# A hybrid attention layer with expert retrieval: 44 scatters per head instead of 48, and a second set of split weights in the activation stage

## The chip, the cores and the metric

One Trainium2 chip, one of its cores. The time of a kernel is the device time of one launch in microseconds (us), and the median of several runs is what counts. Profiles come from one further execution with the hardware profiler on. The engines are TensorE (PE; its weight loads are PEld), VectorE (DVE), ScalarE (ACT), GpSimd (POOL) and SyncE (SP), which only issues transfers here.

## The reference

A layer for 512 tokens and 16 meta tokens at width 2048: 8 heads of stick-breaking attention and 8 of forgetting attention, an output projection, then retrieval of experts by product keys. The last part takes nearly all the time and all of the change:

```python
def block(hb):
    q = (hb @ w_query).reshape(PEER_BLOCK, PEER_HEADS, 2, D_KEY // 2)
    s = jnp.einsum('thpc,hpnc->thpn', q, sub_keys)
    ...
    best_s, best_j = lax.top_k(cand_s, PEER_TOPK)
    idx = jnp.take_along_axis(cand_i, best_j, axis=-1)
    g = jax.nn.softmax(best_s, axis=-1)
    u_sel = jnp.take(u, idx, axis=0)
    a = jax.nn.gelu(jnp.einsum('thkd,td->thk', u_sel, hb), approximate=False)
    v_sel = jnp.take(v, idx, axis=0)
    return jnp.einsum('thk,thkd->td', (g * a).astype(hb.dtype), v_sel)
```

Each token has 8 heads with 16 experts each, out of 16384 = 128 x 128. Everything is float32.

## The kernel before

Float32 products are made from two halves: a weight tile `wr` is cast to a high half `wh` (ScalarE, L190) and the rest `wl` is subtracted (VectorE, or GpSimd where told, L191), and three matmuls give the product.

**Two ways for two kinds of tokens.** The first 160 tokens (128 "full" ones and 32 more, the x set) fetch the rows of their own experts: one gather per expert slot (`ahead`, L844, an indirect DMA on GpSimd's queue, 128 rows of 16 KB with u and v, 2 MB) into `grf`, of which there are two buffers. Then VectorE makes a dot with the token (L858), ScalarE makes the coefficient (L876, L877), and VectorE accumulates the v part (L864). The other 352 tokens (TD) are done densely: all 16384 experts in 128 blocks of 128.

**The stages of the dense part** are a list of items in order. `("A", j)` for j = 26 to 127: 48 matmuls of 352 columns (L1032) into `pa`, GELU on ScalarE (L903), stored to `a_scr`. `("D", j)` for j = 0 to 15: the same, but multiplied with the gate values `gg` read from `g_scr`, split into `ph` and `pl`. Then 256 V items with 24 matmuls each (L1046), between them the R items that bring activations and gates back. In iteration t the kernel issues loads for three items ahead, cuts item t + 1 into halves (`cut_up`) and issues the matmuls of item t. An item's weights are four quarters; `wh` and `wl` have four buffers each, so a quarter of the next item is cut when TensorE has read that quarter of the item before.

**The gate table.** `g_scr` in HBM holds a gate per (expert, dense token). It is zeroed early and filled by scatters: `total` (L951, VectorE) sums the gates of equal experts of a token into one column of `tot`, and a scatter (L963, an indirect DMA on GpSimd's queue) writes the 128 values of a column of `tot` to the places in a column of `dst`. Tokens 128 to 511 are three blocks of 128 (NDB); per head 3 x 16 = 48 columns, 8 heads, so 384 scatters. The first 32 partitions of block 0 are the x set; they need no table, so their `dst` points behind the table. `scatter` is a generator; each step makes one total of head h and one scatter of head h - 1, and iterations take 4 or 5 steps by turns (`NSC`).

**Order.** TensorE, VectorE, ScalarE and SyncE keep the order in which the code is written; GpSimd's queue is ordered by the scheduler when the program is built. In an iteration the steps of the gathers (`due(WA)`) and of the scatters stand between the four splits. Every queue is served in order, so what stands behind a waiting instruction waits too.

Of the kernel before, what the change touches and what calls it, by code (L numbers as in the profile page):

```python
# [9 lines left out]
F32 = mybir.dt.float32  # L10
F32R = mybir.dt.float32r
# [9 lines left out]
P = 128  # L21
# [3 lines left out]
D = 2048  # L25
KD = D // P
NH = 8
NTB = T // P
TOPK = 16
PH = 8  # L30
X = 32
TD0 = P + X
TD = T - TD0
NDB = NTB - 1
NG = P // X
# [6 lines left out]
GATES = 1  # L42
WA = 1.9
JC = 16
LEAD = JC // 2 + 1
NSC = (4, 5)
AHEAD = 3


# [46 lines left out]
def hymba_peer(ctx: ExitStack, tc: tile.TileContext, xT, w_in, w_fl, b_fg, g_mix, g_q, g_k, g_merge,  # L96
               w_out, g_ffn, w_q, keysT, uT, uv, out):
    nc = tc.nc

    def pool(name, bufs=1, **kw):  # L100
        return tc.tile_pool(name=name, bufs=bufs, **kw)

    cst = ctx.enter_context(pool("cst"))
    wp = ctx.enter_context(pool("wp", 3))
# [34 lines left out]
                            base=0, channel_multiplier=1)  # L139
# [4 lines left out]
                            base=-P, channel_multiplier=-1)  # L144
# [3 lines left out]
                            base=0, channel_multiplier=1)  # L148
# [4 lines left out]
                            base=0, channel_multiplier=1)  # L153
# [70 lines left out]
    with ExitStack() as fctx:  # L224
# [9 lines left out]
        with ExitStack() as actx:  # L234
# [16 lines left out]
            for k in range(KD):  # L251
                if k % 8 == 0:
                    wr = wp.tile([P, KD // 2, P], F32, name=f"wr_q0_{k}", tag="wr", bufs=2)
                x = raw.tile([P, S], F32, name=f"xr{k}", tag="raw")
# [8 lines left out]
                if k % 4 == 0:  # L263
                    wh = wp.tile([P, 4, P], F32R, name=f"wh_q0_{k}", tag="wh", bufs=4)
                    wl = wp.tile([P, 4, P], F32R, name=f"wl_q0_{k}", tag="wl", bufs=4)
# [12 lines left out]
                b = big.tile([P, S], F32R, name=f"hl{k}", tag="hl")  # L278
# [11 lines left out]
            for i, (lo, hi) in enumerate(KV):  # L290
                pm = pj(f"pss{i}")
                nc.tensor.matmul(pm[:, :264], ones, ssq[:, lo:hi], start=True, stop=True)
                y = rsqrt(t2, pm[:, :264], D, [P, 264], f"n{i}")
# [349 lines left out]
        with ExitStack() as mctx:  # L643
# [65 lines left out]
            first = [project(w_out[c], mh, ml, [(0, T)], f"wo{c}", hfs=(0,)) for c in range(3)]  # L709
# [178 lines left out]
    def due(n, hold=False):  # L888
        done[1] += n
        want = 0 if hold else min(nwork, int(nwork * done[1] / (0.975 * (WA * (P - NAP - GATES - 1) + 2 * P))))  # L890
        r = range(done[0], max(want, done[0]))
        done[0] = r.stop
        return [gens[i + 1] for i in r]
# [5 lines left out]
    dst = gp.tile([P, NDB, P], I32, name="dst")  # L899
    tot = gp.tile([P, NDB, P], F32, name="tot")  # L900
    def act_out(j, ps, keep=False):
        g = dn.tile([P, TD], F32, name=f"ga{j}", tag="ga", bufs=4)
        nc.scalar.activation(g, ps[:, :TD], AF.Gelu)  # L903
        if keep:
            return g
        nc.sync.dma_start(a_scr[j], g)

    def gates():
        e = gp.tile([P, NTB, P], F32, name="e")
        es = gp.tile([P, 2, NTB * PH], F32, name="es")  # L910
        ev = e.rearrange("p b (h k) -> p (b h) k", k=TOPK)
        nc.scalar.activation(e, res[:, :, 2, :], AF.Exp)
        nc.vector.reduce_sum(es[:, 0], ev, axis=AX.X)
        nc.vector.reciprocal(es[:, 1], es[:, 0])
        nc.vector.tensor_tensor(ev, ev, es[:, 1].unsqueeze(2).to_broadcast([P, NTB * PH, TOPK]), op=OP.mult)
        nc.vector.tensor_copy(g0, e[:, 0, :])
        nc.vector.scalar_tensor_tensor(ef, res[:, :, 1, :], float(P), res[:, :, 0, :], op0=OP.mult, op1=OP.add)
        nc.vector.tensor_copy(idx0, ef[:, 0, :])
        idxt = gp.tile([X, P], I32, name="idxt")
        nc.vector.tensor_copy(idxt, ef[:X, 1, :])  # L920
        for i in range(NG):
            for t, src in ((idx1, idxt), (g1, e[:X, 1, :])):
                nc.sync.dma_start(t[i * X:i * X + X], src[:, i * SL:i * SL + SL])
            nc.sync.dma_start(rxx[i * X:i * X + X], rx)
        for b in range(NDB):
            nc.vector.tensor_scalar(dst[:, b, :], ef[:, b + 1, :], float(TD), tcol[:, b:b + 1], op0=OP.mult, op1=OP.add)
        nc.gpsimd.iota(dst[:X, 0, :], pattern=[[1, P]], base=P * P * TD, channel_multiplier=P)
        return e

    act_out(JC, pa[0])  # L930
# [7 lines left out]
    psO = ctx.enter_context(pool("psO", 1, space=PSUM))  # L938
    wx = ctx.enter_context(pool("wx", 2))
    gt = ctx.enter_context(pool("gt", 2))  # L940
    pq = ctx.enter_context(pool("pq", 2))

# [2 lines left out]
    def scatter():  # L947
        def total(h, b, i):
            s, w = h * TOPK + i, (h + 1) * TOPK
            junk = gp.tile([P, P], F32, name=f"junk{h}{b}{i}", tag="junk")  # L950
            nc.vector.scalar_tensor_tensor(junk[:, :w], ef[:, b + 1, :w], ef[:, b + 1, s:s + 1],  # L951
                                           gts[:, b + 1, :w], op0=OP.is_equal, op1=OP.mult,
                                           accum_out=tot[:, b, s:s + 1])

        slots = [(b, i) for b in range(NDB) for i in range(TOPK)]
        for h in range(PH + 1):
            head = []
            for b, i in slots:
                if h < PH:
                    total(h, b, i)  # L960
                if h > 0:
                    s = (h - 1) * TOPK + i
                    w = nc.gpsimd.indirect_dma_start(  # L963
                        out=g_flat, out_offset=bass.IndirectOffsetOnAxis(ap=dst[:, b, s:s + 1], axis=0),
                        in_=tot[:, b, s:s + 1], in_offset=None)
                    for x in head:
                        tc.declare_no_dep(w.ins, x.ins, reason="the experts of one head differ")
                    head.append(w)
                yield
# [9 lines left out]
                items.append(("R", c * JC + x // 2 + LEAD))  # L979
            items.append(("V", c * JC + jj, half))  # L980

    ga, gg, raw_w, cut, pp, po, ppool = {}, {}, {}, {}, {}, {}, {}
    count = [0, 0]

    def kind(t):
        return items[t][0] if 0 <= t < len(items) else ""

    def load_gates(t):
        if kind(t) not in ("R", "D"):
            return  # L990
        j = items[t][1]
        if kind(t) == "R":
            ga[j] = dn.tile([P, TD], F32, name=f"gb{j}", tag="gb", bufs=3)
            nc.sync.dma_start(ga[j], a_scr[j])
        gg[j] = dn.tile([P, TD], F32, name=f"gg{j}", tag="gg", bufs=3)
        nc.sync.dma_start(gg[j], g_tab[j])

    def load(t):
        if t >= len(items):
            return  # L1000
        it = items[t]
        j = it[1]
        parts = [(f"u{x}", uT[j][:, x * 8:x * 8 + 8, :]) for x in range(2)] if it[0] != "V" else \
            [(f"v{it[2]}", uv[j * P:j * P + P, D + it[2] * H:D + it[2] * H + H])]
        raw_w[it] = []
        for nm, src in parts:
            w = (wp, wx)[count[0] % 2].tile([P, KD // 2, P], F32, name=f"wr_{nm}_{j}", tag="wr", bufs=2)
            count[0] += 1
            nc.sync.dma_start(w if it[0] != "V" else w.rearrange("p a b -> p (a b)"), src)
            raw_w[it].append(w)  # L1010

    def cut_up(it, lo_eng=None, work=()):
        r = []
        for n, w in enumerate(raw_w.pop(it)):
            for x in range(2):
                wh = wp.tile([P, 4, P], F32R, name=f"wh_{it[0]}{n}{x}_{it[1]}", tag="wh", bufs=4)
                wl = wp.tile([P, 4, P], F32R, name=f"wl_{it[0]}{n}{x}_{it[1]}", tag="wl", bufs=4)
                split(wh, wl, w[:, x * 4:x * 4 + 4, :], lo_eng)
                r.append((wh, wl))
                settle()  # L1020
                if it[0] != "V":
                    for _ in range(-(-len(work) // (5 - len(r)))):
                        next(work.pop(0), None)
        cut[it] = r
# [27 lines left out]
        return g  # L1052

    def high(j, g):
        ph = pq.tile([P, TD], F32R, name=f"ph{j}", tag="ph", bufs=2 * LEAD)
        nc.scalar.copy(ph, g)
        return g, ph

    def low(j, g, ph):
        pl_ = pq.tile([P, TD], F32R, name=f"pl{j}", tag="pl", bufs=2 * LEAD)  # L1060
        nc.vector.tensor_tensor(pl_, g, ph.bitcast(F32), op=OP.subtract)
        pp[j] = ph, pl_

# [23 lines left out]
    with tc.manual_schedule(engines=fixed):  # L1087
        sc = scatter()
        loaded = 0
        held = ()  # L1090
        for t in range(len(items) + 1):
            load_gates(t + 3)
            while t < len(items) and loaded < len(todo) and loaded <= rank[t] + AHEAD:
                load(todo[loaded])
# [4 lines left out]
                add_up(prev)  # L1099
            if prev[0] == "A":  # L1100
                act_out(prev[1], ga.pop(prev[1]))
            if prev[0] == "D":
                ga[prev[1]] = act_out(prev[1], ga.pop(prev[1]), True)
                g = gated(prev[1])
                low(prev[1], *high(prev[1], g))
# [3 lines left out]
                gts = gates()  # L1109
            work = []  # L1110
            if kind(t) in ("A", "D") and t > GATES:
                work = due(WA) + [sc] * NSC[t % 2]
            elif kind(t) == "V":
                work = due(1, hold=items[t][1] % JC == JC - 1 and t < len(items) - JC)
            if nxt.get(t) is not None:
# [83 lines left out]
```

## Time and profile before

| | |
|---|---|
| median of 3 runs | 3365.06 us (3356.91 to 3369.4) |
| profiled execution | 3352.32 us, its span 3350.6 us |
| mean TensorE clock granted | 0.987 |
| busy share of the span | PE 97%, PEld 91%, DVE 74%, POOL 42%, ACT 40% |
| A items (1303 to 2202 us) | 899 us of the span |

Busy matmul time overlaps itself, since matmuls are pipelined; what an item costs is read from how many matmuls pass in a stretch. The clock is a share of 2.4 GHz; 0.5 is the lower level of 1.2 GHz. "Idle before" an instruction is time in which its engine did nothing, and the name behind it is what ended that time, as inferred from semaphores.

### The profile page before, as it was taken

The page shows a single profiled execution, that of the slowest core. Times are in us where ns is not written, and L with a number is a line of the kernel's source. Part 1 is how long each engine was busy: PE and PEld are TensorE (multiplying, and loading weights), DVE is VectorE, ACT ScalarE, POOL GpSimd, SP SyncE. Part 2 cuts the span into 40 slices and gives each one's busy share as a digit, 9 for nine tenths or more (in the row PEclk, how much of TensorE's full clock was granted, in tenths as well). Part 3 has the DMA queues.
Part 4 walks back from the last instruction along what each step waited for, and adds up shares of the span by engine and source line. Part 5 has one row for each costly group of instructions (what it writes and reads, how often), then busy time and mean ns, then how long its engine had stood idle before and what let it go on. Part 6 is the DMA issues. An engine that isn't in the chain of part 4 may idle for free.

```text
span 3350.6 us, 52860 instructions
## 1 busy us (share of the span) xinstructions
PE 3240.2 (97%) x19406; PEld 3046.7 (91%) x19406; DVE 2476.6 (74%) x4526; ACT 1349.3 (40%) x2762; POOL 1408.3 (42%) x974
## 2 busy tenths in 40 slices
PE   8999999999999999998989899999999999999998
PEld 6888888897888889998989899999999999999998
DVE  7555565666645997776767777677898889888885
ACT  5445554453333333333333333344333334433332
POOL 2000000003125866887878788112434434334332
PEclk9999999999999999999999999999999999999999
DMA  3332223222443235887888777888999999999994
GB/s 122 123 108 88 103 104 104 104 105 83 139 136 117 95 113 190 315 300 271 297 301 294 280 283 280 348 336 321 400 373 357 371 368 358 369 372 352 364 369 161
DMA packets 210661, 810.83 MB, mean 242 GB/s; under 512 B 35520, under 2 KB 89920, under 8 KB 189376
## 3 DMA queue, kind: packets, MB, share of 16 engines
q1 hardware_dynamic: 169184, 448.60, 37.8%
q0 software_dynamic: 41216, 358.85, 27.4%
q8 instruction: 152, 2.49, 0.3%
q14 instruction: 109, 0.89, 0.1%
HBM read 754.41 MB, written 52.10 MB: 241 GB/s over the span
## 4 chain that ended last, share of the span: by engine, by line
PE 75%; DMA 11%; issue 5%; DVE 5%; POOL 3%; ACT 1%; SPq 0%; DVEq 0%; POOLq 0%; ACTq 0%
PE pv L1046 21%; PE pa L1032 17%; DMA grf<-in_uv_dram,idx 7%; PE pj_wo L219 5%; PE pj_wq L219 5%; PE pj_sv L219 3%; PE pj_fv L219 3%; PE pj_sk L219 3%; PE pj_fk L219 3%; PE pj_fq L219 3%; PE pj_fg L219 3%; DMA wr_v<-in_uv_dram 2%; PE pa L219 2%; PE pj_sq L219 2%; POOL wl_V L191 2%
## 5 line engine op out<-in xcount | busy, mean ns | idle before, releaser
L1046 PE MATMUL pv<-ph,wl_V 128*128 128x352 f32 x2048 | 663.2, 324 | 18.2 <-POOL wl_V L191 13.5
L1046 PE MATMUL pv<-ph,wh_V 128*128 128x352 f32 x2048 | 660.1, 322 | 0.0
L1046 PE MATMUL pv<-pl,wh_V 128*128 128x352 f32 x2048 | 659.9, 322 | 0.0
L1032 PE MATMUL pa<-dh,wl_A 128*128 128x352 f32 x1632 | 545.8, 334 | 69.2 <-DVE wl_A L191 63.7
L963 POOL DMA_INDIRECT g_scr<-tot,dst x384 | 538.7, 1403 | 149.2 <-issue 88.8
L1032 PE MATMUL pa<-dh,wh_A 128*128 128x352 f32 x1632 | 543.0, 333 | 0.0
L1032 PE MATMUL pa<-dl,wh_A 128*128 128x352 f32 x1632 | 536.5, 329 | 0.0
L190 ACT CAST wh_V<-wr_v 128x512 fp32r<-128x512 f32 x512 | 310.9, 620 | 507.9 <-PE pv L1046 345.5
L858 DVE SCALAR_TENSOR_TENSOR grf<-grf,hbn 128x2048 f32<-128x2048 f32 x128 | 304.4, 2378 | 151.7 <-DMA grf<-in_uv_dram,idx 106.6
L1046 PEld LDWEIGHTS pv<-ph,wl_V 128*128 128x128 f32 x2048 | 385.5, 188 | 26.6 <-POOL wl_V L191 20.6
L190 ACT CAST wh_A<-wr_u 128x512 fp32r<-128x512 f32 x408 | 249.8, 617 | 378.8 <-PE pa L1032 297.5
L191 POOL TENSOR_TENSOR wl_V<-wr_v,wh_V 128x512 fp32r<-128x512 f32 x130 | 265.7, 2054 | 313.9 <-ACT wh_V L190 285.7
L1046 PEld LDWEIGHTS pv<-pl,wh_V 128*128 128x128 f32 x2048 | 385.6, 188 | 0.0
L1046 PEld LDWEIGHTS pv<-ph,wh_V 128*128 128x128 f32 x2048 | 385.6, 188 | 0.0
L1032 PEld LDWEIGHTS pa<-dh,wl_A 128*128 128x128 f32 x1632 | 314.9, 193 | 76.0 <-DVE wl_A L191 70.2
L191 DVE TENSOR_TENSOR wl_V<-wr_v,wh_V 128x512 fp32r<-128x512 f32 x382 | 285.6, 779 | 104.8 <-ACT wh_V L190 93.9
L191 DVE TENSOR_TENSOR wl_A<-wr_u,wh_A 128x512 fp32r<-128x512 f32 x404 | 277.4, 690 | 107.9 <-ACT wh_A L190 78.6
L844 POOL DMA_INDIRECT grf<-in_uv_dram,idx x128 | 184.9, 1445 | 394.3 <-DVE acc L864 346.6
L864 DVE SCALAR_TENSOR_TENSOR acc<-grf,coef,acc 128x2048 f32<-128x2048 f32 x128 | 309.1, 2415 | 14.9 <-ACT coef L877 12.0
L1032 PEld LDWEIGHTS pa<-dh,wh_A 128*128 128x128 f32 x1632 | 316.7, 194 | 0.0
L1032 PEld LDWEIGHTS pa<-dl,wh_A 128*128 128x128 f32 x1632 | 315.8, 193 | 0.0
L355 POOL TENSOR_TENSOR osq<-o 128x512 f32<-128x512 f32 x14 | 14.5, 1036 | 527.1 <-ACT o L349 527.1
(405 smaller groups left out, 6677.1 us busy)
## 6 DMA issues: line engine op xcount, KB each, us to landing
wr_u<-in_uT_dram SPq DMA_DIRECT2D x256, 512.0 KB
wr_v<-in_uv_dram SPq DMA_DIRECT2D x256, 512.0 KB
g_scr<-zero POOLq DMA_DIRECT2D x16, 1408.0 KB
gg<-g_scr SPq DMA_DIRECT2D x128, 176.0 KB
a_scr<-ga SPq DMA_DIRECT2D x112, 176.0 KB
gb<-a_scr SPq DMA_DIRECT2D x112, 176.0 KB
wr_wo<-in_w_out_dram SPq DMA_DIRECT2D x32, 512.0 KB
wr_wq<-in_w_q_dram SPq DMA_DIRECT2D x32, 512.0 KB
```

Source lines behind the costliest of these rows:

```text
L190: nc.scalar.copy(hi, src)
L191: (lo_eng or nc.vector).tensor_tensor(lo, src, hi.bitcast(F32), op=OP.subtract)
L219: nc.tensor.matmul(ps[i][:, :hi - lo], wt[:, kk, :], ht[k][:, lo:hi], start=(k == 0 and n == 0), stop=(k == KD - 1 and n == 2))
L355: nc.gpsimd.tensor_tensor(sq, r, r, op=OP.mult)
L844: nc.gpsimd.indirect_dma_start(out=r, out_offset=None, in_=uv, in_offset=bass.IndirectOffsetOnAxis(ap=sets[st][3][:, s:s + 1], axis=0))
L858: nc.vector.scalar_tensor_tensor(r[:, :D], r[:, :D], 1.0, hb, op0=OP.mult, op1=OP.mult, accum_out=dt[:, c])
L864: nc.vector.scalar_tensor_tensor(ac, r[:, D:], cf[:, c], ac, op0=OP.mult, op1=OP.add)
L963: w = nc.gpsimd.indirect_dma_start(out=g_flat, out_offset=bass.IndirectOffsetOnAxis(ap=dst[:, b, s:s + 1], axis=0), in_=tot[:, b, s:s + 1] ...
L1032: nc.tensor.matmul(ps[:, :TD], wt[:, k % 4, :], ht[k], start=(k == 0 and n == 0), stop=(k == KD - 1 and n == 2))
L1046: nc.tensor.matmul(po["now"][n][:, :TD], w_, a, start=(jj == 0 and pi == 0), stop=(jj == JC - 1 and pi == 2))
```

## The change

The 32 idle partitions of block 0 take over the last four columns (`MOVED`) of block 2: four small copies per head on SyncE's queue put 32 partitions by 4 values each into `tot[:32, 0]` (`borrowed`), and four copies at the start do the same with `dst`. So 12 scatters of block 2 and 44 in all are left per head. Totals are now made for blocks 1, 2 and 0 in this order, the copies follow the head's last total, and block 0's scatters come after them. For the first head only every second slot is a step. The number of steps per iteration comes from `nsc`, which deals them over the iterations up to four items ahead of the first D item.

A pool `wy` is opened in the space that `ph` and `pl` take from the D stage on: it holds two more raw tiles and a second set of four `wh` and four `wl`, used by A items with odd j. It is closed at the first D item, where the pool `pq` is opened.

```diff
-NSC = (4, 5)
+MOVED = TOPK // NG
...
+    def borrowed(t, heads, q):
+        return t[:X, 0].rearrange("p (h q m) -> p h q m", q=NG, m=MOVED)[:, heads, q]
...
-        nc.gpsimd.iota(dst[:X, 0, :], pattern=[[1, P]], base=P * P * TD, channel_multiplier=P)
+        for q in range(NG):
+            nc.sync.dma_start(borrowed(dst, slice(0, PH), q),
+                              dst[q * X:q * X + X, NDB - 1].rearrange("p (h s) -> p h s", s=TOPK)[:, :, TOPK - MOVED:])
...
-    pq = ctx.enter_context(pool("pq", 2))
+    wyx = ExitStack()
+    ppool = {"wy": wyx.enter_context(pool("wy", 4))}
...
-        slots = [(b, i) for b in range(NDB) for i in range(TOPK)]
+        slots = [(b, i) for b in (*range(1, NDB), 0) for i in range(TOPK)]
         for h in range(PH + 1):
             head = []
-            for b, i in slots:
+            for n, (b, i) in enumerate(slots):
                 if h < PH:
                     total(h, b, i)
+                if h < PH and n == len(slots) - 1:
+                    for q in range(NG):
+                        nc.sync.dma_start(
+                            borrowed(tot, slice(h, h + 1), q),
+                            tot[q * X:q * X + X, NDB - 1, None, h * TOPK + TOPK - MOVED:h * TOPK + TOPK])
+                if b == NDB - 1 and i >= TOPK - MOVED or h == 0 and n % 2 == 0:
+                    continue
...
+    first = items.index(("D", 0)) - 4
+    nscat = PH * (NDB * TOPK - MOVED) + NDB * TOPK // 2 + 1
+
+    def nsc(t):
+        return -(-nscat * (min(t, first) - GATES) // (first - GATES))
...
-            w = (wp, wx)[count[0] % 2].tile([P, KD // 2, P], F32, name=f"wr_{nm}_{j}", tag="wr", bufs=2)
+            w = (wp, wx, ppool["wy"])[count[0] % (3 if it[0] == "A" else 2)].tile(
+                [P, KD // 2, P], F32, name=f"wr_{nm}_{j}", tag="wr", bufs=2)
...
-                wh = wp.tile([P, 4, P], F32R, name=f"wh_{it[0]}{n}{x}_{it[1]}", tag="wh", bufs=4)
-                wl = wp.tile([P, 4, P], F32R, name=f"wl_{it[0]}{n}{x}_{it[1]}", tag="wl", bufs=4)
+                b = ppool["wy"] if it[0] == "A" and it[1] % 2 else wp
+                wh, wl = (b.tile([P, 4, P], F32R, name=f"{y}_{it[0]}{n}{x}_{it[1]}", tag=y, bufs=4)
+                          for y in ("wh", "wl"))
...
+            if prev[0] == "A" and kind(t) == "D":
+                wyx.close()
+                ppool["pq"] = ctx.enter_context(pool("pq", 2))
...
-                work = due(WA) + [sc] * NSC[t % 2]
+                work = due(WA) + [sc] * (nsc(t) - nsc(t - 1))
```

GpSimd's queue of the kernel before, about a third of the way through the scatters (`grf` rows are gathers, the `g_scr` rows runs of scatters):

```order
L844 DMA grf_16135<-in_uv_dram,idx_8879 128x4096
L963 DMA g_scr<-tot,dst 5771264x1 x4
L844 DMA grf_16228<-in_uv_dram,idx_8879 128x4096
L963 DMA g_scr<-tot,dst 5771264x1 x9
L844 DMA grf_16405<-in_uv_dram,idx_8879 128x4096
L963 DMA g_scr<-tot,dst 5771264x1 x9
L844 DMA grf_16495<-in_uv_dram,idx_8879 128x4096
L963 DMA g_scr<-tot,dst 5771264x1 x4
L844 DMA grf_16672<-in_uv_dram,idx_8879 128x4096
L963 DMA g_scr<-tot,dst 5771264x1 x10
L844 DMA grf_16765<-in_uv_dram,idx_8879 128x4096
```

Between two gathers stand 4 and 9 or 10 scatters by turns, nowhere none. The same part of GpSimd's queue in the changed kernel, in which the scatters have the line L978:

```order
L844 DMA grf_16198<-in_uv_dram,idx_8879 128x4096
L844 DMA grf_16288<-in_uv_dram,idx_8879 128x4096
L844 DMA grf_16459<-in_uv_dram,idx_8879 128x4096
L978 DMA g_scr<-tot,dst 5771264x1 x17
L844 DMA grf_16553<-in_uv_dram,idx_8879 128x4096
L978 DMA g_scr<-tot,dst 5771264x1 x3
L844 DMA grf_16727<-in_uv_dram,idx_8879 128x4096
L978 DMA g_scr<-tot,dst 5771264x1 x11
L844 DMA grf_16817<-in_uv_dram,idx_8879 128x4096
L978 DMA g_scr<-tot,dst 5771264x1 x3
```

Here three gathers follow each other with no scatter between them, then 17 scatters stand before the next gather; this is the place at which a head ends. Runs of 17 or 18 stand three times in the whole queue, runs of 12 to 14 seven times, and 13 pairs of neighbouring gathers have one scatter or none between them. SyncE's queue of the changed kernel where the first head ends (`wr_u` are weight loads, `a_scr` the stores of activations, `tot<-tot` the new copies):

```order
L906 DMA a_scr<-ga_14324 128x352
L1032 DMA wr_u_36_14409<-in_uT_dram 128x1024
L1032 DMA wr_u_36_14411<-in_uT_dram 128x1024
L906 DMA a_scr<-ga_14413 128x352
L971 DMA tot<-tot 32x4 x4
L1032 DMA wr_u_37_14504<-in_uT_dram 128x1024
L1032 DMA wr_u_37_14506<-in_uT_dram 128x1024
L906 DMA a_scr<-ga_14508 128x352
```

The four copies stand between the store of one iteration and the weight loads of the next; before, the loads followed the store at once.

## Rows read from the trace of the kernel before

**Rows 1.** windows, 1303 to 2202 us: length, busy time of five engines, clock, DMA share, GB/s.
```profile
1303.00:2107.00 804.00, 735.28 (x4321) 728.92 (x4320) 574.36 (x1306) 276.95 (x567) 620.48 (x446) 0.95 0.80 289
2107.00:2202.00 95.00, 94.47 (x579) 94.11 (x578) 66.61 (x72) 36.56 (x76) 11.39 (x8) 1.00 0.89 343
```

**Rows 2.** waits of TensorE, 1300 to 2205 us: total, times, longest.
```profile
PE pa L1032 <- DVE wl_A L191: 63.7, 19, 6.4
PE pa L1032 <- DVE junk L951: 5.3, 1, 5.3
```

**Rows 3.** timeline of TensorE around 1560 us: start, length, instruction, idle time before it.
```profile
1558.25 0.33 PE L1032 MATMUL pa<-dh,wh_A 128*128 128x352 f32 x1
1558.42 0.32 PE L1032 MATMUL pa<-dl,wh_A 128*128 128x352 f32 x1
1563.70 0.66 PE L1032 MATMUL pa<-dh,wl_A 128*128 128x352 f32 x1 [4.97 <-DVE wl_A L191]
1564.16 0.49 PE L1032 MATMUL pa<-dh,wh_A 128*128 128x352 f32 x1
1564.45 0.49 PE L1032 MATMUL pa<-dl,wh_A 128*128 128x352 f32 x1
```

**Rows 4.** groups by line, 1333 to 2107 us, in which the scatters are issued.
```profile
L963 POOL DMA_INDIRECT g_scr<-tot,dst x384 | 538.7, 1403 | 149.2 <-issue 88.8 <-DVE junk L951 35.0 <-DMA g_scr<-tot,dst 15.7
...
L190 ACT CAST wh_A<-wr_u 128x512 fp32r<-128x512 f32 x348 | 213.1, 617 | 320.4 <-PE pa L1032 256.2 <-issue 28.3 <-DVE junk L951 15.7
...
L858 DVE SCALAR_TENSOR_TENSOR grf<-grf,hbn 128x2048 f32<-128x2048 f32 x56 | 128.1, 2288 | 128.6 <-DMA grf<-in_uv_dram,idx 85.1 <-issue 43.5
L951 DVE SCALAR_TENSOR_TENSOR junk<-ef,e 128x16 f32<-128x16 f32 (+7 forms) x383 | 110.7, 289 | 2.4
L844 POOL DMA_INDIRECT grf<-in_uv_dram,idx x57 | 76.1, 1336 | 21.5 <-issue 10.1 <-DVE junk L951 5.2 <-DVE acc L864 4.4
```

**Rows 5.** timeline of VectorE, 1547 to 1569 us.
```profile
1547.06 2.35 DVE L864 SCALAR_TENSOR_TENSOR acc<-grf,coef,acc 128x2048 f32<-128x2048 f32 x1 [0.60 <-ACT coef L876]
...
1560.55 2.29 DVE L858 SCALAR_TENSOR_TENSOR grf<-grf,hbn 128x2048 f32<-128x2048 f32 x1 [7.54 <-issue]
...
1565.94 2.35 DVE L864 SCALAR_TENSOR_TENSOR acc<-grf,coef,acc 128x2048 f32<-128x2048 f32 x1
```

**Rows 6.** timeline of GpSimd, 1547 to 1562 us.
```profile
1550.56 1.41 POOL L844 DMA_INDIRECT grf<-in_uv_dram,idx  x1 [0.30 <-DVE junk L951]
1552.27 0.97 POOL L963 DMA_INDIRECT g_scr<-tot,dst  x1 [0.30 <-DVE wl_A L191]
...
1557.38 0.98 POOL L844 DMA_INDIRECT grf<-in_uv_dram,idx  x1 [0.30 <-issue]
...
1561.27 2.41 POOL L963 DMA_INDIRECT g_scr<-tot,dst  x1 [0.36 <-DMA g_scr<-tot,dst]
```

**Rows 7.** chain of waits, 1300 to 2350 us: start, length, what.
```profile
1517.44 12.02 DMA grf<-in_uv_dram,idx
...
1590.08 10.23 DMA grf<-in_uv_dram,idx
1600.31 1.55 issue
```

**Rows 8.** timeline of GpSimd after the last scatter.
```profile
2106.19 0.98 POOL L844 DMA_INDIRECT grf<-in_uv_dram,idx  x1 [4.37 <-DVE acc L864]
...
2129.62 2.75 POOL L844 DMA_INDIRECT grf<-in_uv_dram,idx  x1 [13.65 <-DVE acc L864]
```

**Rows 9.** gathered rows' tile, 2107 to 2330 us: lengths, first and last start.
```profile
L858 DVE SCALAR_TENSOR_TENSOR grf<-grf,hbn x19: 2283/2286/2293, 2107.3 to 2327.5; 128x2048 f32<-128x2048 f32 x19
```

**Rows 10.** timeline of SyncE's DMA issues at the start of the activation stage.
```profile
1325.42 0.57 SPq L924 DMA_DIRECT2D rxx<-rx  x1
1331.56 0.51 SPq L923 DMA_DIRECT2D idx<-idxt  x1
1335.88 0.51 SPq L923 DMA_DIRECT2D g<-e  x1
```

More of the change, by code (lines that the diff above doesn't have):

```diff
@@ L980, in hymba_peer @@
             items.append(("V", c * JC + jj, half))
-    ga, gg, raw_w, cut, pp, po, ppool = {}, {}, {}, {}, {}, {}, {}
+    ga, gg, raw_w, cut, pp, po = {}, {}, {}, {}, {}, {}
     count = [0, 0]
@@ L1054, in high @@
     def high(j, g):
-        ph = pq.tile([P, TD], F32R, name=f"ph{j}", tag="ph", bufs=2 * LEAD)
+        ph = ppool["pq"].tile([P, TD], F32R, name=f"ph{j}", tag="ph", bufs=2 * LEAD)
         nc.scalar.copy(ph, g)
@@ L1059, in low @@
     def low(j, g, ph):
-        pl_ = pq.tile([P, TD], F32R, name=f"pl{j}", tag="pl", bufs=2 * LEAD)
+        pl_ = ppool["pq"].tile([P, TD], F32R, name=f"pl{j}", tag="pl", bufs=2 * LEAD)
         nc.vector.tensor_tensor(pl_, g, ph.bitcast(F32), op=OP.subtract)
@@ L1091, in hymba_peer @@
         for t in range(len(items) + 1):
+            if t == first + 1:
+                assert next(sc, None) is None and sc.gi_frame is None
             load_gates(t + 3)
```

## The prediction

> **What bounds the kernel now.** I read the stretches first, then TensorE's waits, then who feeds the engine that it waits for. The activation stage (items A 26 to 127, 102 of them) lasts 899 us: 804 us in which scatters are issued and 95 us without [rows 1]. In the second part the clock is 1.00 and 579 matmuls pass in 95 us, 0.164 us each, so an item of 48 costs 7.88 us and 102 items would cost 803 us. The stage therefore loses 96 us, all of it while scatters run; that is everything the change could win there. Of it TensorE stands still for 63.7 + 5.3 = 69 us, in 20 waits, nearly all for the low halves from VectorE [rows 2]; most of the rest is clock: after a wait of 4.97 us the matmuls come every 0.29 us instead of 0.17 us, the lower of the two levels, 1.2 against 2.4 GHz [rows 3]; the mean clock of the 804 us is 0.95 [rows 1].
>
> VectorE is late because it stands before a dot (L858) whose gathered row has not landed: 128.6 us of idle time before 56 dots [rows 4]. One case: dot at 1560.55 after 7.54 us of idle time; its gather was issued at 1550.56, 10.0 us before [rows 5, 6]. In the chain two more are seen: 12.02 us, and 10.23 + 1.55 = 11.8 us [rows 7]. I take 11.3 us from issue to dot.
>
> And the gathers are late because GpSimd's queue is full. Between 1333 and 2107 us it issued 384 scatters and 57 gathers, 441 in 774 us, **1.755 us each** [rows 4]. Undisturbed, one takes 0.97 us and a pause of 0.30 us, 1.27 us together; one beside the dot of 1560.55 takes 2.41 us [rows 5, 6]. The rest, 0.485 us per DMA or 3.75 us per gather's share of 7.74 DMAs, is what VectorE's work for one gather stretches. A gather's buffer is free when the accumulate two gathers back ends; the one of 1557.38 was issued 8.0 us after that (1547.06 + 2.35 = 1549.41) [rows 5, 6]. After the last scatter each gather goes out as an accumulate ends, with GpSimd idle for 4 to 14 us before it [rows 8], and dots come every (2327.5 - 2107.3)/18 = 12.2 us [rows 9]: the pace that TensorE at full speed allows. So the first part is bound by GpSimd's queue, not by the buffers of the split.
>
> **A sum that gives back the kernel before.** I carry the stage from gather to gather with three rules: a gather is issued 1.755 us per DMA after the one before it, but not before the accumulate two gathers back ended; its dot starts 11.3 us later, but not sooner than 12.2 us after the dot before; the accumulate ends 7.7 us after the dot's start (1560.55 to 1565.94 + 2.35) [rows 5]. In the order of before, 9 to 11 and 3 to 5 scatters alternate. A pair of 10 and 4 costs (11 + 5) x 1.755 = 28.1 us where 24.4 are to be had, 3.7 us lost. Over the 60 gathers to the last scatter the sum loses 85 us; measured are 96, so 1 us of the sum counts 1.13 us.
>
> **The change, part by part.**
>
> Scatters: 352 instead of 384. 32 x 1.755 = 56 us of GpSimd's time go. By itself, spread evenly, that takes a 60-gather stretch from 444 x 1.755 = 779 us to 723 us, under the 732 us of 60 dots: the loss would be gone.
>
> But it is not spread evenly on GpSimd's queue, which isn't ordered by hand. Block 0's scatters now need the head's last totals and four copies, so all 16 come at a head's end, and while block 0's totals are made there is nothing to scatter. The order shows three gathers with no scatter between them, then 17 scatters, then the next gather; later 18, and 18 again, and elsewhere 12 to 14, seven times. The same three rules, for 18: gather c is issued at time T, when an accumulate ends; its dot is 8.0 us short of two paces later, T + 16.4, and the next gather's dot is wanted at T + 28.6. That gather is issued at T + 19 x 1.755 = T + 33.3 and lands for a dot at T + 44.6: **16 us lost in one burst**. In the empty stretch before it GpSimd could have worked, but it stood at a gather that waited for its buffer; this time doesn't come back. Over the 60 gathers the new order loses 143 us by 1.755 us per DMA. In a burst VectorE only has two gathers' work, so the price falls to (19 x 1.27 + 2 x 3.75)/19 = 1.66 us; at that the order loses 117 us. I take 130, between them: 130 - 85 = 45, times 1.13, **+51 us**. At 1.27 throughout, the lower end, it would lose 26; at 1.55 it equals before.
>
> The wait at a head's end: the rules let scatters start at once. The first one of block 0 stands in the queue until the last total is made and the four copies on SyncE's queue have landed; the rest of that queue, the next gather included, stands behind it. The trace has no such copy. The nearest rows are the small copies at the start of the stage, which SyncE issues 0.5 to 0.6 us long, and of which two were held, 5.6 us (1325.99 to 1331.56) and 3.8 us [rows 10]. Ends: nothing, or 9.4 us in each of 8 heads, 75 us. I take 4 us, one issue after the other plus a short hold: **+32 us**. The weight loads behind the copies are three items ahead, 24 us, and hide it.
>
> The second set of split weights lets ScalarE and VectorE cut an item while TensorE still reads the one before. What it can save is lead: at most one item, 7.88 us, and then again as far as VectorE earns it back. VectorE works 574 us for 57 gathers, 10.1 us in a pace of 12.2 [rows 1]; but each of its dots stands in order before the next cut and waits for a gather issued no sooner than the release, so a faster VectorE meets the landing 11.3 us later. Ends: nothing, or 7.88 us at each of 8 heads, 63 us. I take one item in all, **-8 us**.
>
> Totals: as many as before (384 at 289 ns [rows 4]), two to a slot at times; they stay below VectorE's 2.1 us of spare time per gather, so nothing. The four copies of dst and the absent iota come once, about 2 us beside TensorE's work; if that cover is gone, 2 us. The third pair of raw buffers brings loads forward; no wait of TensorE's names a load [rows 2]. The space of the gated values is opened after the last A item, whose successor's gate product comes a whole D item later, 7.88 us of cover. The D and V stages keep their code.
>
> Sum: 51 + 32 - 8 = **+75 us** on the profiled execution's 3352.3 us, 3427 us. Its median of runs is 3365, 13 us above, in a spread of 12 us; I add 1 us and no more: **3428 us**.
>
> What speaks for a cheaper burst: the Trainium skill, "SBUF — State Buffer", Who interferes with whom, says that a two-input VectorE instruction takes only the read side of the port pair that GpSimd shares, and infers that descriptor generation wants the write side. By it a scatter would cost 1.27 us beside dots too and the new order would lose 26 us instead of 130, about 3310 us. The trace disagrees: 2.41 us beside one [rows 6].
>
> **Rivals.**
>
> *The second set carries TensorE over the bursts: faster.* Waits below one item vanish; of the 18 in my sum at 1.66 those above 7.88 us (14.2 twice, 12.6, 12.1, 8.7) leave 22 us, so 85 - 22 = 63, times 1.13, is 71 us less: 3281 us, or about 3300 with the copies. It needs the lead to be whole again before each burst, 7.88 us in some 7 gathers, 1.1 of the 2.1 us that VectorE has to spare for each. For: the cut waits 256 us for TensorE now [rows 4]. Against: in the slow part VectorE sits idle for gathers, not for buffers. The Trainium skill, "Perfetto Trace Analysis", Optimization Strategy, says that bubbles which repeat on the engine that should be full can mean too few buffers for the next tile; by that rule this rival holds, and its time is the one above. 0.09.
>
> *Bursts at the undisturbed price: faster.* 26 to 74 us lost (1.27 to 1.5 us per DMA) instead of 85, with no hold of the copies: 3285 to 3340, middle 3310. It decides below 1.55 us. 0.05.
>
> *Nothing moves.* 1.55 us in the bursts and copies that land in time: the gain and the loss of GpSimd meet, 3352 to 3365. 0.09.
>
> *SyncE is held by its copies and the weight loads behind it come late.* The 75 us end of the copies on top of 143 - 85: 3352 + 66 + 75 = 3493 and above. For: the held copies at the stage's start [rows 10]. Against: only four stand in a row here, there twelve. 0.05.
>
> *The forecast's mechanism*, bursts and empty stretches on GpSimd's queue: 0.72, from 3385 (30 us, the 1.66 end and no hold) to 3480.
>
> **How the numbers follow.** No change is within 0.5%, 17 us, of 3365, about what this measurement can tell. Faster 0.14, same 0.09, slower 0.77. The likeliest case alone spans 3385 to 3480. The range reaches down to 3350 to take in the case that nothing moves, so 0.72 + 0.09, and leaves out the faster ones and SyncE's.
>
> **What would show it.** GpSimd's rows: 352 scatters, runs of 17 and 18 without a gather among them, 20 us and more between two gathers there; GpSimd idle before gathers because of an accumulate, and before a scatter because of a copy or a total, tens of us each where now there is nearly none. VectorE: fewer idle times before dots, but of 10 us and more. TensorE: waits for the low halves of over 10 us, 100 us and more in all, last scatter after 2150 us, activation stage 960 to 1000 us. The D and V stages the same to a few us. I am wrong if TensorE's waits in the activation stage fall below 69 us, or if the gathers behind the bursts go out less than 8 us after their buffer is free.

## The result and the profile after

The changed kernel takes 3420.77 us (median; 3417.34 to 3422.11), the kernel before 3363.46 us on the same chip: a ratio of 1.0169, 95% interval 1.0148 to 1.019: slower by 1.7%. The forecast was 3428 us. The profiled execution has a span of 3419.2 us against 3350.6, 68.6 us more.

First the stretches after (columns as in [rows 1]): while scatters are issued, the rest of the activation stage, both together, and the D items.

```profile
1303.00:2176.00 873.00, 750.17 (x4360) 742.71 (x4360) 578.29 (x1315) 259.64 (x575) 546.69 (x412) 0.92 0.75 271
2176.00:2269.40 93.40, 90.51 (x545) 90.22 (x544) 60.13 (x67) 31.10 (x69) 13.87 (x10) 0.98 0.88 330
1303.00:2269.40 966.40, 840.68 (x4903) 832.93 (x4903) 638.42 (x1381) 290.74 (x644) 560.57 (x421) 0.93 0.77 277
2269.40:2395.70 126.30, 125.69 (x770) 125.30 (x769) 100.50 (x123) 53.96 (x113) 11.44 (x10) 1.00 0.86 319
```

The activation stage lasts 966 us where it lasted 899, and loses 163 us against the 803 us of TensorE at full speed, where it lost 96. GpSimd is busy less (547 us in 873, before 620 in 804 [rows 1]) and yet done later. The clock falls from 0.95 to 0.92. The D items take 126 us, before 127, and V differs by 2 us.

What TensorE and GpSimd wait for in the stage (total, times, longest):

```profile
PE pa L1056 <- DVE wl_A L191: 121.6, 22, 15.3
PE pa L1056 <- ACT wh_A L190: 3.7, 2, 3.4
PE pa L1056 <- issue: 0.3, 1, 0.3
```

```profile
POOL grf L844 <- DVE acc L864: 108.1, 12, 16.8
POOL g_scr L978 <- issue: 81.4, 265, 1.0
POOL g_scr L978 <- DMA tot<-tot: 80.3, 7, 17.2
POOL grf L844 <- DVE junk L959: 55.1, 15, 11.9
```

TensorE's waits went from 69 us in 20 [rows 2] to 126 us in 25, and a longest one of 6.4 us became one of 15.3. GpSimd now stands 80 us before a scatter whose value a copy (`tot<-tot`) brings; before it had no such wait. One of the seven shows what follows. GpSimd, then SyncE, then VectorE, then TensorE (timelines; columns as in [rows 3]):

```profile
1587.49 1.33 POOL L844 DMA_INDIRECT grf<-in_uv_dram,idx  x1 [11.52 <-DVE junk L959]
1601.99 2.63 POOL L978 DMA_INDIRECT g_scr<-tot,dst  x1 [13.17 <-DMA tot<-tot]
...
1625.03 0.96 POOL L978 DMA_INDIRECT g_scr<-tot,dst  x1 [0.30 <-issue]
1626.30 0.97 POOL L978 DMA_INDIRECT g_scr<-tot,dst  x1 [0.30 <-issue]
1627.57 0.98 POOL L844 DMA_INDIRECT grf<-in_uv_dram,idx  x1 [0.30 <-issue]
```

```profile
1590.61 3.77 SPq L971 DMA_DIRECT2D tot<-tot  x4
1594.48 2.08 SPq L1032 DMA_DIRECT2D wr_u<-in_uT_dram  x2
```

```profile
1593.57 0.27 DVE L959 SCALAR_TENSOR_TENSOR junk<-ef,e 128x48 f32<-128x48 f32 x1
...
1599.20 2.35 DVE L864 SCALAR_TENSOR_TENSOR acc<-grf,coef,acc 128x2048 f32<-128x2048 f32 x1
1601.46 2.29 DVE L858 SCALAR_TENSOR_TENSOR grf<-grf,hbn 128x2048 f32<-128x2048 f32 x1
...
1635.47 2.29 DVE L858 SCALAR_TENSOR_TENSOR grf<-grf,hbn 128x2048 f32<-128x2048 f32 x1 [20.51 <-DMA grf<-in_uv_dram,idx]
```

```profile
1623.03 0.32 PE L1056 MATMUL pa<-dl,wh_A 128*128 128x352 f32 x1
1638.63 0.66 PE L1056 MATMUL pa<-dh,wl_A 128*128 128x352 f32 x1 [15.28 <-DVE wl_A L191]
```

Read it downwards. The first of the four copies is issued at 1590.61. The head's last total (48 columns wide) ends at 1593.84, and the fourth copy, which needs it, is issued by 1594.38. The first scatter of block 0 starts at 1601.99, 11.4 us after the first copy was issued; that copy is the one it waits for (last section). From there to the next gather stand 17 scatters, 25.6 us, 1.50 each. The gather behind them goes out at 1627.57, 26.0 us after its buffer came free (1601.55). So VectorE stands still for 20.5 us, and TensorE for 15.3.

### The profile page after: what moved, and what is told of

Its sections match the earlier page's. It is cut to its first block, busy times and chain, and to the rows that moved or that the text cites. A ratio compares the mean times of both kernels' runs of the same rounds, so it can differ in the third digit from the quotient of the medians.

```text
span 3419.2 us, 52546 instructions
## 1 busy us (share of the span) xinstructions
PE 3250.8 (95%) x19406; PEld 3055.0 (89%) x19406; DVE 2472.9 (72%) x4526; ACT 1327.0 (39%) x2762; POOL 1324.9 (39%) x941
## 5 line engine op out<-in xcount | busy, mean ns | idle before, releaser
L978 POOL DMA_INDIRECT g_scr<-tot,dst x352 | 469.5, 1334 | 205.4 <-issue 81.4
L844 POOL DMA_INDIRECT grf<-in_uv_dram,idx x128 | 174.0, 1360 | 484.7 <-DVE acc L864 376.3
L864 DVE SCALAR_TENSOR_TENSOR acc<-grf,coef,acc 128x2048 f32<-128x2048 f32 x128 | 309.4, 2417 | 12.6 <-ACT coef L877 11.4
L876 ACT ACTIVATE coef<-dots 128x1 f32<-128x1 f32 x160 | 32.4, 202 | 542.8 <-DVE grf L858 504.1
L190 ACT CAST wh_A<-wr_u 128x512 fp32r<-128x512 f32 x408 | 227.3, 615 | 8.4 <-PE pa L219 5.0
```

Of the source, the lines that this page charges most:

```text
L190: nc.scalar.copy(hi, src)
L844: nc.gpsimd.indirect_dma_start(out=r, out_offset=None, in_=uv, in_offset=bass.IndirectOffsetOnAxis(ap=sets[st][3][:, s:s + 1], axis=0))
L864: nc.vector.scalar_tensor_tensor(ac, r[:, D:], cf[:, c], ac, op0=OP.mult, op1=OP.add)
L876: nc.scalar.activation(cf, dt, AF.Gelu)
L978: w = nc.gpsimd.indirect_dma_start(out=g_flat, out_offset=bass.IndirectOffsetOnAxis(ap=dst[:, b, s:s + 1], axis=0), in_=tot[:, b, s:s + 1] ...
```

## The experiments

Pinning means that each gather stays behind the scatters written ahead of it, and each scatter behind the gather; GpSimd's queue is otherwise ordered by the scheduler. Ratios are to the kernel before on the same chip.

| kernel | median us | ratio (95%) | stage us | TensorE waits us |
|---|---|---|---|---|
| before | 3363 | 1 | 899 | 69 |
| changed | 3421 | 1.0169 (1.0148 to 1.019) | 966 | 126 |
| e1, one set | 3467 | 1.03 (1.0267 to 1.0333) | 999 | 158 |
| e2, before with two sets | 3367 | 1.0008 (0.9991 to 1.0025) | 905 | 76 |
| e3, no copies | 3329 | 0.9889 (0.9861 to 0.9917) | 872 | 51 |
| e4, pinned | 3309 | 0.9833 (0.9799 to 0.9868) | 852 | 33 |
| e5, before pinned | 3376 | 1.0036 (1.0021 to 1.0051) | 917 | 80 |
| e7, quarters | 3357 | 0.9978 (0.9967 to 0.999) | 898 | 72 |
| e8, pinned, dealt by gather | 3281 | 0.9756 (0.9732 to 0.9779) | 819 | 12 |
| e9, bunched, no copies | 3396 | 1.0089 (1.0057 to 1.012) | 935 | 107 |
| e10, e8 with one set | 3294 | 0.9793 (0.9773 to 0.9813) | 835 | 22 |
| e11, 48 dealt as in e8 | 3335 | 0.991 (0.989 to 0.9931) | 880 | 52 |
| e12, bunched and held | 3448 | 1.0249 (1.0223 to 1.0274) | 990 | 157 |
| e13, e12 without copies | 3387 | 1.0075 (1.005 to 1.01) | 930 | 101 |

The stage runs from the first matmul of A's weights after 1290 us to the last one. The theory is the prediction's, called Q in the expectations: bunches of scatters on GpSimd's queue make gathers late. Its rivals are that the second set costs or wins much, that the number of scatters costs, and that the copies' holds cost whatever the order.

**e1, the scatters without the second set.** The edit takes the weights from `wp` and `wx` again:

```diff
...
-                b = ppool["wy"] if it[0] == "A" and it[1] % 2 else wp
-                wh, wl = (b.tile([P, 4, P], F32R, name=f"{y}_{it[0]}{n}{x}_{it[1]}", tag=y, bufs=4)
-                          for y in ("wh", "wl"))
+                wh = wp.tile([P, 4, P], F32R, name=f"wh_{it[0]}{n}{x}_{it[1]}", tag="wh", bufs=4)
+                wl = wp.tile([P, 4, P], F32R, name=f"wl_{it[0]}{n}{x}_{it[1]}", tag="wl", bufs=4)
```

> The changed kernel with its 44 scatters per head and the copies, but the activation stage cuts its weights into one set of halves, as in the kernel before. Theory Q (the bunches of scatters on GpSimd's queue cost the time): still slower than before. The order on GpSimd's queue comes out with runs of 18, 16, 17, 16, 16 and 16 scatters between two gathers, more of them than in the changed kernel; the three rules give a loss of 160 to 188 us against 117 to 145, so 3425 to 3480 us. Rival S (the second set and its loads are what costs): about 3365 us or less. Rival L (the second set is worth a good deal): 30 us and more above what the bunches alone explain, over 3480.

Measured 3467 us, in Q's range. It can't price the set, since the scheduler's order on GpSimd changed too and has more long runs.

**e2, the second set without the scatters.** The kernel after with the scatter part of before: old `slots`, no copies, the iota, steps of 4 and 5.

> The kernel before with the second set of halves alone: 48 scatters per head in its even order, no copies. Theory Q: VectorE still stands before its dots for late gathers and a lead of one item is used up once; 0 to 10 us are won, 3355 to 3368 us, and TensorE's waits for the low halves stay at 50 to 70 us. Rival S: the set costs, 3390 to 3430 us. Rival L (the prediction's first rival, the set carries TensorE over the bunches): waits below one item of 7.88 us go, 3300 us or less.

No difference that can be told, and none of the up to 10 us that Q allowed; TensorE's waits, 75 us, lie above the 50 to 70 expected. Its rows (ScalarE's group, idle time behind the last bar; TensorE's waits):

```profile
L190 ACT CAST wh_A<-wr_u 128x512 fp32r<-128x512 f32 x369 | 205.3, 615 | 1.4 <-PE pa L219 1.4
```

```profile
PE pa L1047 <- DVE wl_A L191: 75.3, 20, 7.7
```

The cuts no longer wait for TensorE (256 us in [rows 4], 1.4 here), so the set does what it says; TensorE waits as long as before. The buffers of the halves were not what bound the stage.

**e3, no copies.** The four copies of `tot` and the four of `dst` go, the iota comes back; the last four columns of block 2 are left out of the computation.

> The changed kernel without the twelve small copies per head (four of the totals, and the four of the positions at the stage's start, for which the iota comes back): block 0's scatters no longer need the head's last totals. It leaves out the last four columns of block 2, whose gates reach no place that is right. Number of scatters, order in which they are written and second set are those of the changed kernel. Theory Q: with nothing held to the head's end the order has 8 to 9 and 3 to 4 scatters between gathers, only the first head has runs of 13 and 15; the three rules give 20 to 34 us of loss against 87 of before, so 3285 to 3310 us. Rival C (the count of scatters or their new pairing with totals costs, or the second set): no faster than 3400.

The copies that go are four per head and four once, not twelve per head. 3329 us, faster than before by 1.1%, where the expected range ended at 3310. With nothing held to the head's end the scheduler deals 7 to 9 and 3 to 4 scatters between gathers, but for the first head, which has three runs of 13 to 15. The sign and the mechanism hold; the size fell short by some 20 us.

**e4, the changed kernel pinned.** The whole change stays; edges of issue order are added, first the helper, then what stands behind the issue `w` of a gather and of a scatter:

```diff
+    since = []
+
+    def behind(w, those):
+        for x in those:
+            tc.add_manual_dep(w.ins, x.ins.name, reason="issue order", info=mybir.DependencyInfo(
+                mybir.DependencyClass.NoSync, mybir.DependencyReason.DATA))
...
+            behind(w, since)
+            since[:] = [w]
...
+                    behind(w, since[:1])
+                    since.append(w)
```

> The changed kernel, all of it, with one thing added: on GpSimd's queue each gather stays behind the scatters written ahead of it and each scatter behind the gather written ahead of it, so that 8 and 4 scatters alternate with gathers throughout. Same scatters, same copies, same second set. Theory Q: at 1.755 us per DMA a pair of gathers takes 24.6 us where 24.4 are to be had; the three rules lose 1 to 5 us, and a copy issued at a head's end has some eight gathers' time until its scatters come, so the holds go too: 3265 to 3285 us. Rival H (the holds of the copies on SyncE's queue, or what they do to the weight loads, cost the time whatever the order): 3340 to 3420. Rival S: 3380 and above.

3309 us: the order alone takes 1.0169 to 0.9833, 113 us. That shows Q most plainly, since every scatter, copy and buffer of the change is still there; bunches and waits for copies go together. The forecast of 3265 to 3285 was too good by 24 us. GpSimd's waits, first of e4, then the last of these of e8 below:

```profile
POOL grf L851 <- DVE acc L873: 194.4, 27, 14.2
POOL g_scr L987 <- issue: 103.4, 336, 0.7
POOL grf L851 <- DVE junk L968: 25.7, 13, 15.3
POOL g_scr L987 <- DMA g_scr<-tot,dst: 23.1, 11, 6.6
```

```profile
POOL g_scr L987 <- DMA g_scr<-tot,dst: 18.1, 11, 4.4
```

Hardly any scatter waits for a copy any more. But scatters wait for earlier ones to land, 23 us, by the expectation of e8 at the start of a new head (called old-head waits here). They don't account for what is left: e8 has nearly the same and is 28 us faster.

**e5, the kernel before pinned.** The same edges on the old code.

> The kernel before, with GpSimd's queue pinned as in e4: gathers and scatters stay in the order in which they are written, 9 and 4 or 5 scatters alternating, where they were 9 to 11 and 3 to 5. Theory Q: the queue of before was nearly even already; the three rules give 45 to 86 us of loss against 48 to 87, so no change that can be told, 3355 to 3370 us. Rival P (pinning itself wins time, whatever the order, and e4's gain came from it): 3310 us or less.

Slower by 0.36%, 5 us over the range of Q, so pinning by itself wins nothing: e4's gain came from the order that it restored. Why e5 loses 12 us is open; the old-head waits are 24.9 us here, 15.7 before.

**e7, copies by quarters.** A repair without pinning:

```diff
+        slots = [(NDB - 1, i) for i in range(keep, TOPK)] + [(0, i) for i in range(TOPK)] + \
+            [(1, i) for i in range(TOPK)] + [(NDB - 1, i) for i in range(keep)]
...
-                if h < PH and n == len(slots) - 1:
-                    for q in range(NG):
+                if h < PH and b == 0 and i % MOVED == MOVED - 1:
+                    for q in (i // MOVED,):
```

> The changed kernel with its totals in another order and GpSimd's queue left to the scheduler: block 2's four moved columns come first, then block 0, and after every four columns of block 0 the one copy that feeds them, so that block 0's scatters come free in fours. Theory Q: the order has 8 and 3 to 4 scatters between gathers, up to 16 in the first head only; the rules lose 28 to 51 us against 20 to 34 of the kernel without copies, which took 3329, so 3330 to 3350 us. Rival H (a copy's hold on SyncE's queue costs wherever it stands): the holds come as often as before, 3375 and more.

3357 us, between the two ranges: GpSimd's waits for copies fell from 80 to 18.6 us, but SyncE now stands 30 times, 181 us in all, at a copy that waits for a total, with weight loads behind it; in the changed kernel it is 8 times, 26 us. Whether that costs the rest was not tried.

**e8, six scatters between any two gathers.** e4 with the steps of `scatter` dealt by VectorE's steps on the gathered rows:

```diff
-                work = due(WA) + [sc] * (nsc(t) - nsc(t - 1))
+                work = mixed(due(WA), t)
...
+        for n, x in enumerate(gens_):
+            upto = done[0] - len(gens_) + n + 1
+            k = min(nscat, -(-nscat * upto // halves))
+            r += [x] + [sc] * (k - paid[0])
...
```

The lines of the loop are from `mixed`: behind each half step of a gather (`x`) come as many scatter steps as bring their count up to its share. As a step also makes a total, VectorE's totals are spread evenly with the scatters.

> e4 with the scatters dealt by VectorE's steps on the gathered rows instead of by items, so that 6 scatters stand between any two gathers where 8 and 4 alternate. Theory Q: a gather behind 8 scatters went out 8 to 10 us after its buffer was free; behind 6, at 1.755 us, 7 DMAs are 12.3 us, one pace, so nothing is lost but where a new head's scatters wait for the old head's to land (23 us in e4 on GpSimd): 3285 to 3303 us against e4's 3309. Rival V (six totals of VectorE in a row ahead of a cut hold TensorE): 3312 and more. If e4's rest has another cause, the same as e4 within 6 us.

3281 us, 4 us under the range of Q and faster than both kernels: 2.4% below the one before. The stage's row (columns as in [rows 1]) and TensorE's waits:

```profile
1303.00:2122.80 819.80, 807.83 (x4902) 805.62 (x4901) 640.23 (x1381) 292.35 (x645) 593.29 (x421) 0.99 0.91 325
```

```profile
PE pa L1082 <- DVE wl_A L191: 11.8, 5, 5.2
```

12 us of waits are left of 126, the clock is 0.99, and the stage is 16 to 17 us over the 803.

**e9, bunches without copies.** e3 and pinned; block 0's 16 scatters written together:

```diff
+                if b == 0 and i < TOPK - 1:
+                    yield
+                    continue
+                for i in (range(TOPK) if b == 0 else (i,)) if h > 0 else ():
```

> The kernel without copies (e3; it leaves out the last four columns of block 2), pinned as in e4, but block 0's 16 scatters written all at once at the end of their head's turn: runs of 16 to 21 scatters, seven in all, with empty stretches before them, and no copy and no hold. It tells the price of the bunches from that of the holds, which the prediction put at 51 and 32 us. Theory Q: the rules lose 111 to 140 us against 117 to 145 for the changed kernel, so by the prediction's terms its time less the holds, 3385 to 3400 us. If the holds cost nothing of their own: 3405 to 3425. If the holds are most of the loss: 3365 us or less.

3396 us, in the range of the prediction's terms: bunches alone make the kernel slower than before, and by the ratios 27 us less slow than the change.

**e10 and e11, the parts of the change under an even deal.** e10 is e8 with e1's edit; e11 puts e8's two edits on the kernel before (its first head also takes a step for every second slot only, as in the change).

> e8 (6 scatters between any two gathers) with one set of halves in the activation stage instead of two: the price of the second set where nothing is bunched. By the prediction's term of 8 us: 3284 to 3295 us against e8's 3281. If the second set is worth nothing: within 5 us of e8. If it is worth a good deal once the queue is even (it covers the short waits that are left): 3300 and more.

> The kernel before, with all its 48 scatters per head, its iota and its one set of halves, pinned and dealt by VectorE's steps as in e8: 6 and 7 scatters alternate between gathers. It tells the price of the four scatters per head from that of their order. Theory Q with the count: 7.5 DMAs at 1.66 to 1.755 us are 12.5 to 13.2 us against a pace of 12.2; the rules lose 10 to 49 us against none for e8, so 3290 to 3330 us. If order is all and the count nothing: 3275 to 3290.

By the ratios, from two chips, e10 is 0.37% (about 12 us, give or take 10) slower than e8: that is what the second set is worth, once nothing is bunched. e11 less e10 is 1.17%, about 39 us (give or take 10): what four scatters fewer per head are worth, the copies that replace them included. e11 is 5 us over its range, and 0.9% under the kernel before: the even deal helps there too.

**e12 and e13, the holds.** Block 0's scatters stand right behind the head's end, with the copies (e12) and without (e13; the last four columns of block 2 left out):

```diff
+                if b == 0 and n < len(slots) - 1:
+                    yield
+                    continue
+                if b == 0:
+                    head = opened
+                for g, i in [(h, x) for x in range(TOPK) if h < PH] if b == 0 else [(h - 1, i)] if h > 0 else ():
+                    s = g * TOPK + i
```

> The changed kernel, pinned, with block 0's 16 scatters written right behind the four copies at their head's end, where they wait for them, the gathers behind them: runs of 16 to 21 scatters, eight in all, and the hold of the copies as in the changed kernel. Theory Q: the rules lose 113 to 131 us without the holds; e13's time and the holds on top, 20 to 35 us, so 3400 to 3430 us.

> e12 without the copies (it leaves out the last four columns of block 2; the iota is back): the same order on GpSimd's queue, the bunches at the same places, behind the same last totals of VectorE, and nothing on SyncE to wait for. Theory Q: 3375 to 3400 us, near the 3396 of e9. The difference of e12 and e13 is the price of the holds alone: 32 us by the prediction, about 25 by the difference of the changed kernel and e9; under 8 us, if the holds only lie in time that the bunches lose anyway.

e13 lies in its range, e12 18 us above. GpSimd's waits, first of e12, then of e13:

```profile
POOL grf L851 <- DVE acc L873: 169.7, 17, 14.4
...
POOL g_scr L993 <- DMA tot<-tot: 72.2, 7, 14.1
```

```profile
POOL grf L851 <- DVE acc L873: 223.3, 23, 14.5
...
POOL g_scr L986 <- DVE junk L966: 5.8, 19, 0.3
```

Without the copies nothing stands before the bunch but totals, for which e13's scatters hardly wait. The copies cost 1.74%, about 58 us (46 to 70) in eight heads, 7 us a head.

## Why the prediction was right, point by point

**The bound: right.** The stage is bound by when GpSimd's queue lets the gathers out. e4 changes only that order and wins 113 us against the changed kernel; e8, which spreads VectorE's totals as well, wins 139. The loss of 96 us that the prediction called all that could be won is real: e8 wins 80 of it.

**An even spread would make the loss go: nearly.** The prediction's aside, 60 gathers in 723 us of DMA, is e8: 16 us of loss are left.

**The bunches: right in kind, not separable to the microsecond.** The runs of 17 and 18 stand where the order shows them, and behind them the gathers go out 26.0, 20.4 and 19.8 us after their buffers are free. The price per DMA, put at 1.66 us in a run, is 1.50, 1.66 and 1.62 in the three (start of the first scatter to that of the gather, by their number), and 1.67 over all thirteen runs of 10 and more. It splits as the sum had it: in the run above the last twelve scatters take 0.96 to 1.10 us, nearly all with VectorE idle, and the first, beside the dot of 1601.46, 2.63. Of all 352, the 124 during which VectorE did nothing took 0.97 us, and the 114 that ran for over 0.2 us beside a dot or an accumulate of gathered rows 1.91 in the mean. The Trainium skill, "SBUF — State Buffer", Who interferes with whom, infers that a two-input instruction of VectorE leaves descriptor generation alone; the trace disagrees here too. e9 and e13, bunched and without copies, are 30 and 25 us slower than before; the term was 51. So the term looks too large by 21 to 26 us, but this is not settled: their runs stand elsewhere than those of the change, and they have the second set.

**The rules: good for bunches, too kind otherwise.** By the expectations they give 111 to 140 us for e9, whose stage lost 132 against 803, and 113 to 131 for e13, which lost 127. For evener orders they give 1 to 5 for e4, which lost 49, 10 to 49 for e11, which lost 77, and none for e8, which lost 16. The correction is thus no factor of 1.13: 16 to 44 us are lost there that the rules don't hold, and what they are is open.

**The holds: right in place, wrong in what is waited for, small in size.** The prediction let the first scatter of block 0 wait for the last total and all four copies, 4 us a head. It waits for the first copy alone, 5.3 to 11.4 us from that copy's issue (last section), most of it the landing, for which the term had little room. e12 less e13 gives 7 us a head, 58 us where the term was 32. In the changed kernel itself the difference to e9 and e13 is 27 and 32 us by the ratios; but the runs stand elsewhere in those two. GpSimd's idle time before such scatters is no price by itself: e12 has 72 us of it, and e13, without copies, waits 54 us longer for accumulates before its gathers instead.

**The second set: right.** Nothing on the kernel before (e2), 12 us where nothing is bunched (e10), against 8. The rival that it carries TensorE over the bunches is refuted by e2 and by the changed kernel: ScalarE waits for TensorE no more, TensorE waits longer. The Trainium skill, "Perfetto Trace Analysis", Optimization Strategy, says that repeated bubbles can mean too few buffers; here the buffers were given, and the bubbles stayed.

**The sum: +75 us; profile to profile +68.6, by medians +57.** It was 6 to 18 us too large, and its closeness is partly luck. Two terms look wrong in opposite ways, the bunches too large and the holds, by e12 and e13, too small; and the sum was added to a profiled execution of 3352 us, 11 below the median of before, which brought 3428 near 3421.

Of the checks, the last scatter at 2174, waits of TensorE over 10 us and 126 in all, the stage of 966 us and nearly unchanged D and V came as said. One did not: VectorE has not fewer idle times before its dots but more and longer ones, 225 us in 32 up to 2176 us against 136 in 27 up to 2107. First before, then after:

```profile
DVE grf L858 <- DMA grf<-in_uv_dram,idx: 93.0, 17, 9.5
...
DVE grf L858 <- issue: 43.5, 10, 8.5
```

```profile
DVE grf L858 <- DMA grf<-in_uv_dram,idx: 199.9, 28, 20.5
...
DVE grf L858 <- issue: 25.5, 4, 8.1
```

**The other rivals.** Bursts at the undisturbed price and "nothing moves" fail with 1.67 us per DMA in the long runs, above the 1.55 that decides. SyncE's loads behind the copies were not late: ScalarE's cuts wait 3.4 us for them in all.

## What to carry to other kernels

Taking work off the engine that feeds the bound is worth something only if what is left is spread: four scatters fewer per head were worth 39 us in an even order, and the change cost 57 in the order that the scheduler made of their new dependency. The dependency leaves room for the even order, as e4 shows. When a change holds back part of a queue's work until an event, write out the order in which the queue will then serve it, and give the held work its place by hand; here that turned +57 us into -84. Before adding buffers, look what the late engine itself waits for: a second set of halves changed who waited, not how long.

## What was not expected of the hardware

**A tiny copy can land late.** A copy here is 32 partitions by 4 values, half a KB. In the head shown, 11.4 us pass from the issue of the first copy (1590.61) to the start of the scatter that it holds (1601.99); in the seven heads with such a wait it is 5.3 to 11.4 us. In the last head that scatter (second row) starts before the head's last total (third row) is made and before the last copy is issued, at 2147.7, so it waits for neither:

```profile
L971 SPq DMA_DIRECT2D tot<-tot x4: 507/550/593, 2140.2 to 2147.7; - x4
```

```profile
2145.54 1.44 POOL L978 DMA_INDIRECT g_scr<-tot,dst  x1 [14.70 <-DMA tot<-tot]
```

```profile
2147.32 0.35 DVE L959 SCALAR_TENSOR_TENSOR junk<-ef,e 128x128 f32<-128x128 f32 x1
```

The copy's size is not what takes the time. In the head shown the DMA engines are full from 1590.6 to 1598 us, with the gather on GpSimd's queue (`q0`) and with transfers on SyncE's (`q1`; packets, MB, share of the 16 engines):

```profile
q0 software_dynamic: 131, 2.05, 67.0%
q1 hardware_dynamic: 265, 0.90, 33.0%
```

The 128 packets of 16 bytes of the four copies start only between 1598.25 and 1600.56 us.

**A gather lands sooner behind a long run of scatters.** The sum took 11.3 us from a gather's issue to its dot. Of the 32 dots for which VectorE stood idle, the ten behind 12 or more scatters came 8.4 us after their gather in the mean (7.9 in the head shown, 1627.57 to 1635.47), the other 22 came 11.2 us after. Why is not shown.
